# Layer 0 of a two-layer encoder: the Fourier input U taken in one folded pass at the end of the input projection

## The chip, the core and the metric

The kernel runs on one core of one Trainium2 chip. The metric is device time in microseconds (us) for one execution of the whole program; smaller is better. The program before takes 1407.87 us, the median of three runs (1405.26 to 1408.24).

## What is computed

Two layers (`DEPTH` 2) over 512 tokens of width 2048, in float32. Each layer makes shift, scale and gate from a condition vector `c`, normalises the tokens, projects them by `w_in`, mixes one half of the result with a Fourier transform and the other half with latent attention, and projects back by `w_out`:

```python
mod = c_act @ w_ada[l] + b_ada[l]
shift, scale, gate = jnp.split(mod, 3, axis=-1)
h = _layernorm(x) * (1.0 + scale[:, None, :]) + shift[:, None, :]
p = h @ w_in[l]
u_f, z_f, cq, ckv, k_r, z_a = jnp.split(p, split_pts, axis=-1)
y_f = _fourier_mix(u_f, w_fmix[l]) * jax.nn.silu(z_f)
...
y = jnp.concatenate([y_f, y_a], axis=-1) @ w_out[l]
x = _layernorm(DEEPNORM_ALPHA * x + gate[:, None, :] * y, ln_g[l], ln_b[l])
```

`_fourier_mix` takes the real part of a transform over the 512 tokens and the 128 channels of each of 8 groups, and then one 128 x 128 map per group. `w_in` has 3904 columns: 1024 of U (`u_f`), 1024 of ZF (`z_f`, the gate of the Fourier half), 512 of CQ, 320 of CKV with the rotary key, and 1024 of ZA (the gate of the attention half). The real part of a transform of real data is even, so tokens t and 512-t enter only by their sum and difference, and likewise channels c and 128-c. "Folded" means that sums and differences are formed first, which halves the products.

## The kernel before

**Products.** Every float32 product is made of three TensorE matmuls (`mm3`, lines 149 to 152): each operand is split into a rounded high part (`split`, line 146, a cast on ScalarE) and the rest (line 147, a subtraction on VectorE). A block of weights therefore costs a DMA, a ScalarE cast, a VectorE subtraction and matmuls. Blocks come through a `Stream` of units in program order, with two units converted and four loaded ahead (`st`), three raw buffers (`wrp`) and 35 buffers of 4 KB per partition (`bp`).

**Condition vectors.** `w_ada` (50 MB a layer) is not multiplied on TensorE. VectorE adds each row of a loaded tile, times one element of `c_act`, into an accumulator (`ada`, lines 244 and 246). The generator `background` holds this work in due order: shift and scale of layer 0 by blocks of 128 columns, layer 0's gate, then layer 1. `bg_step(n)` lets n pieces through, and the numbers ZP, ZL, AP and CP say how many per unit of weights in the steps of the projection, in the last step, in attention and in the output projection. The tiles are loaded into six buffers (`adp`); 160 pieces of 1024 columns have to be done by the end of layer 0.

**Input projection, layer 0.** The blocks of 128 input features are taken in five steps of 1, 2, 3, 4 and 6 (`SZ`), because a block's `h` needs its shift and scale. In each step all eight groups of columns (UA and UB, the two halves of U, then CQ, CKV, two of ZF, two of ZA) are multiplied by the step's blocks. UA stays in its four PSUM banks through all steps (`keep`); every other group is added to a sum in SBUF after each step (line 1120, VectorE). In the last step the order is UA, CQ, CKV, UB, ZF, ZA. U is folded over tokens after the projection (`folded`), and the transform (`fourier`, called through `pieces`) is dealt out between matmuls of the following groups, as are the latents (`latent_q`, `latent_kv`) and the rotary queries. The ZF gate is applied at once (`gate_f`).

**Input projection, layer 1.** All blocks are ready, and U is folded before the product: `fold_unit` forms sums and differences of weight columns (lines 397, 398) and a product for the token that has no partner (line 408), `u_pass` multiplies 16 blocks of sums and differences of tokens, `folded_constants` and `fourier_folded` make the transform, and `gates` applies ZF, which waited in DRAM (`szd`). Another group of matmuls runs between the pieces of the transform.

**Afterwards.** `project`, `scores`, `probs_T` and `weighted` are attention over 16 half heads; then the output projection in four groups of 512 columns (`residual`, line 1222, and `finish_rows`).

**Order.** A scheduler fixes each engine's instruction order, that of the DMA queues too, when the program is built; at run time every engine takes its instructions in that order and waits at each for what it needs.

## Time and profile before

| what | value |
|---|---|
| median of three runs | 1407.87 us (1405.26 to 1408.24) |
| the profiled execution: its time, its span | 1404.26 us, 1402.5 us |
| TensorE (PE) busy | 1344.3 us, 96% of the span |
| VectorE (DVE) busy | 1015.6 us, 72% |
| ScalarE (ACT) busy | 579.6 us, 41% |
| DMA | 253.24 MB, 181 GB/s over the span |
| step 4 of layer 0 begins on PE | at about 251 us |
| first maximum of layer 0's scores on DVE | at 436.95 us |

The profiled execution is 3.6 us below the median of the three runs. Busy time of an engine is the union of its instructions; durations of instructions overlap a little, so that the distance between two starts is less than a duration. Times in the trace count from the start of the span. The profile names a helper's line for each instruction, so that tiles and shapes tell which work it is: `acc<-ada` is the condition product, `b<-wr` a weight split, `b<-b,pm` with line 1120 a sum over steps.

### The profile page before, as it was taken

Reading aid. Unit: us, or ns where it says so; the run is one execution under the profiler, and the core shown is the slowest. Engines: PE = TensorE matmul, PEld = TensorE weight load, DVE = VectorE, ACT = ScalarE, POOL = GpSimd, SP = SyncE. Lnnn points to the kernel's source line nnn. Section 1 sums busy time; section 2 is a strip of 40 time slices with the busy share of each in tenths; the row PEclk is TensorE's granted clock in tenths of the full one; section 3 lists DMA queues with packets and bytes.
Section 4 is the critical chain, followed back from the end, with each engine's and each line's share of the span. In section 5 each row is a group of like instructions: output and inputs, shape, how many; then the busy total and the mean of one; then the engine's idle time right before and its main releaser. Section 6 shows DMA issues by size and latency. Waiting matters only on the chain. (4 is left out here: it accounts for less than half of the span.)

```text
span 1402.5 us, 18691 instructions
## 1 busy us (share of the span) xinstructions
PE 1344.3 (96%) x6949; PEld 1141.2 (81%) x6949; DVE 1015.6 (72%) x1670; ACT 579.6 (41%) x1052; POOL 55.5 (4%) x82
## 2 busy tenths in 40 slices
PE   4899999999999999999988999998999999999996
PEld 3688888787888888788877888887898888888885
DVE  7899999849978986658588748567655576642448
ACT  6722332224437776112167524323234677721210
POOL 1000000000000000000030001011000000000001
PEclk9999999999999999999998999999999999999998
DMA  9988898824764444968336435369444221263323
GB/s 288 299 293 300 271 349 286 306 76 122 211 206 140 157 128 161 317 199 283 105 145 203 161 96 166 105 205 367 152 119 121 74 67 54 80 236 105 91 60 120
DMA packets 134546, 253.24 MB, mean 181 GB/s; under 512 B 19308, under 2 KB 50168, under 8 KB 134456
## 3 DMA queue, kind: packets, MB, share of 16 engines
q1 hardware_dynamic: 127416, 228.73, 50.1%
q0 software_dynamic: 7040, 23.34, 4.9%
q8 instruction: 54, 0.88, 0.3%
q14 instruction: 36, 0.29, 0.1%
HBM read 237.32 MB, written 14.70 MB: 180 GB/s over the span
## 5 line engine op out<-in xcount | busy, mean ns | idle before, releaser
L150 PE MATMUL pa<-b,b 128*128 128x512 f32 (+4 forms) x1432 | 537.4, 377 | 11.6 <-ACT b L146 5.5
L151 PE MATMUL pa<-b,b 128*128 128x512 f32 (+4 forms) x1432 | 535.9, 375 | 4.3 <-DVE ln_v L187 4.3
L152 PE MATMUL pa<-b,b 128*128 128x512 f32 (+4 forms) x1432 | 534.5, 374 | 1.9 <-DVE b L147 1.9
L146 ACT CAST b<-wr 128x1024 fp32r<-128x1024 f32 (+3 forms) x184 | 180.0, 988 | 356.1 <-PE pa L152 181.1
L150 PEld LDWEIGHTS pa<-b,b 128*128 128x128 f32 x1432 | 271.2, 190 | 59.7 <-ACT b L146 9.2
L151 PEld LDWEIGHTS pa<-b,b 128*128 128x128 f32 x1432 | 272.1, 190 | 48.1 <-DVE ln_v L187 4.6
L152 PEld LDWEIGHTS pa<-b,b 128*128 128x128 f32 x1432 | 271.5, 190 | 48.2 <-DVE b L147 2.9
L147 DVE TENSOR_TENSOR b<-wr,b 128x1024 fp32r<-128x1024 f32 (+3 forms) x184 | 208.1, 1141 | 136.5 <-PE pa L151 84.7
L246 DVE SCALAR_TENSOR_TENSOR acc<-ada,cact,acc 128x1024 f32<-128x1024 f32 (+2 forms) x193 | 227.2, 1184 | 23.1 <-DMA ada<-in_w_ada_dram 21.2
L150 PE MATMUL pm<-b,b 128*128 128x512 f32 (+3 forms) x594 | 201.7, 341 | 1.2 <-ACT b L146 0.8
L151 PE MATMUL pm<-b,b 128*128 128x512 f32 (+3 forms) x594 | 197.2, 333 | 0.0
L152 PE MATMUL pm<-b,b 128*128 128x512 f32 (+3 forms) x594 | 197.0, 333 | 0.0
L150 PEld LDWEIGHTS pm<-b,b 128*128 128x128 f32 x594 | 111.7, 189 | 17.8 <-ACT b L146 2.7
L151 PEld LDWEIGHTS pm<-b,b 128*128 128x128 f32 x594 | 112.3, 189 | 10.5
L152 PEld LDWEIGHTS pm<-b,b 128*128 128x128 f32 x594 | 112.2, 189 | 10.4
L146 ACT CAST b<-pm 128x512 fp32r<-128x512 f32 (+4 forms) x110 | 54.9, 530 | 72.6 <-PE pm L800 17.8
L147 DVE TENSOR_TENSOR b<-pm,b 128x512 fp32r<-128x512 f32 (+4 forms) x110 | 64.1, 610 | 23.6 <-ACT b L146 23.0
L1120 DVE TENSOR_TENSOR b<-b,pm 128x512 f32<-128x512 f32 (+1 forms) x88 | 55.5, 656 | 4.5 <-PE pm L152 4.1
L146 ACT CAST b<-t 128x512 fp32r<-128x512 f32 (+1 forms) x73 | 35.9, 525 | 31.4 <-PE pm L151 9.5
L1039 DVE TENSOR_REDUCE mx<-pa 128x1 f32<-128x512 f32 x64 | 42.9, 684 | 5.3 <-PE pa L1037 4.7
L1044 ACT ACTIVATE t<-t,ssum 128x512 f32<-128x512 f32 x64 | 45.9, 735 | 1.2 <-DVE ssum L1043 1.2
L1042 ACT ACTIVATE t<-pa,mx 128x512 f32<-128x512 f32 x64 | 44.0, 693 | 4.6 <-DVE mx L1039 4.5
(186 smaller groups left out, 1120.7 us busy)
## 6 DMA issues: line engine op xcount, KB each, us to landing
wr<-in_w_in_dram SPq DMA_DIRECT2D x105, 512.0 KB, 4.6
ada<-in_w_ada_dram SPq DMA_DIRECT2D x96, 512.0 KB, 5.3
wr<-in_w_out_dram SPq DMA_DIRECT2D x64, 512.0 KB, 4.1
ada<-in_w_ada_dram SPq DMA_DIRECT2D x96, 256.0 KB, 4.9
ada<-in_w_ada_dram POOLq DMA_DIRECT2D x32, 512.0 KB, 5.4
b<-in_x_dram SPq DMA_DIRECT2D x16, 512.0 KB, 6.3
ada<-in_w_ada_dram SPq DMA_DIRECT2D x32, 192.0 KB, 5.3
wr<-in_w_q_b_dram SPq DMA_DIRECT2D x48, 128.0 KB, 3.0
```

Source lines behind the costliest of these rows:

```text
L146: A.copy(hi, src)
L147: V.tensor_tensor(lo, src, f(hi), op=ALU.subtract)
L150: PE.matmul(o, lh, rh, start=first, stop=False)
L151: PE.matmul(o, lh, rl, start=False, stop=False)
L152: PE.matmul(o, ll, rh, start=False, stop=last)
L246: V.scalar_tensor_tensor(out=a, in0=t[:, r - r0], scalar=cact[:, r:r + 1], in1=a, op0=ALU.mult, op1=ALU.add)
L1039: V.reduce_max(mx, ps, axis=AX.X, negate=True)
L1042: A.activation(e, ps, AF.Exp, bias=mx, accum_out=ssum)
L1044: A.activation(e, e, AF.Copy, scale=ssum)
L1120: V.tensor_tensor(s_[tb], s_[tb], banks[tb][:, :n], op=ALU.add)
```

## The change

In layer 0 U leaves the five steps. The steps multiply six groups; CQ instead of UA stays in banks until the last step (`FIRST`, `LAST`), from where ScalarE copies it out (`latent`). The tokens' transposed `xT` tiles are kept until the end. After the last step, 16 fold units follow; each one first makes its block of token sums and differences (`first_eo`, as the `act` of `fold_unit`), four units ahead (`UA0`). Then `u_pass` runs on all 16 blocks, and `fourier_folded` alternates with the rotary queries. Both gates go to DRAM and ZF comes back in `gates` during attention, where the splits of the Fourier result begin four rounds later (`YS`). The constants of the transform hold four of the six `adp` buffers in layer 0. The pace of the condition products is set anew: fewer in the projection, more in attention and in the output projection. The first residual waits for the gate vector by `gates_done`. `fourier_weights`, `fourier`, `folded`, `gate_f`, `silu` and `pieces` fall away. The diff, cut to its core:

```diff
-    ZP, ZL, AP, CP, G0, G1 = 0.5, 1.0, 1.0, 1.4, 0.8, 1.6
+    ZP, ZL, AP, CP, G0, G1 = 0.3, 0.5, 1.2, 2.3, 0.8, 1.6
...
-    FW, UAH = 2, 6
+    FW, UAH, UA0, YS = 2, 6, 4, 4
...
-    def fold_unit(src, k):
+    def fold_unit(src, k, act=None):
...
         def conv(t):
+            if act is not None:
+                h[k] = act(k)
...
-    FIRST = [UA, UB, CQ, CKV] + ZF + ZA
-    LAST = [UA, CQ, CKV, UB] + ZF + ZA
+    FIRST = [CQ, CKV] + ZF + ZA
+    LAST = [CQ, CKV] + ZA + ZF
...
+            for k in range(NK):
+                st.add(fold_unit(w_in[l], k, lambda k: first_eo(k)))
+            for k in range(2):
+                st.add(wq_unit(l, 4 * k, 4, 128, 64))
...
-            if n[0] <= 6:
+            if n[0] <= (6 if l else 4):
                 return adp.tile(shape, dt, tag="ada", name=nm("fc"))
...
+    def first_eo(k):
+
+        t, v = t2([P, S]), t2([P, S])
+        A.activation(t, xT[k // 2][:, k % 2], AF.Identity, scale=modT[0][:, 16 + k:17 + k], bias=modT[0][:, k:k + 1])
+        V.tensor_tensor(v[:, 0:256], t[:, 0:256], t[:, 256:512], op=ALU.add)
+        V.tensor_tensor(v[:, 256:512], t[:, 0:256], t[:, 256:512], op=ALU.subtract)
+        A.copy(orow[:, k:k + 1], v[:, 256:257])
+        hk = big([P, 2, S])
+        split(hk[:, 0], hk[:, 1], v)
+        return hk
...
-                pace = left[0] / (8.0 * len(pairs(k0, nk)) * LEADS[step])
+                pace = left[0] / (6.0 * len(pairs(k0, nk)) * LEADS[step])
...
-                fa = fourier(0, folded(k_group(UA, keep)))
-                pq = k_group(CQ, [pm() for _ in range(NT)])
...
+                lq = latent_q(k_group(CQ, keep))
                 next(lq)
...
+                lkv = latent_kv(k_group(CKV, pas(), runner(lq)))
                 next(lkv)
...
+                for i, (g, dst) in enumerate(zip(LAST[2:], (0, 1, 2, 3))):
+                    if i == 3:
+                        finish_late()
+                        st.ahead(4, UA0)
+                    zs = k_group(g, pas(), runner(lkv) if i == 0 else lambda: None)
+                    for j in range(4):
+                        A.activation(zs[j], zs[j], AF.Silu)
+                    spill(dst, zs)
+                drain(lkv)
+                cw, nq, dt = folded_constants(0)
+                u = u_pass()
+                st.ahead(4, 2)
+                fb, rq = fourier_folded(u), rotary_queries(1)
+                for i in range(8):
+                    next(fb, None)
+                    next(rq, None)
+                    next(fb, None)
                 drain(fb)
...
+                gt = gates()
...
-            if i < 4:
-                for k in range(2 * i, 2 * i + 2):
+            next(gt, None)
+            next(gt, None)
+            if YS <= i < YS + 4:
+                for k in range(2 * (i - YS), 2 * (i - YS) + 2):
...
-                if l == 1 and g == 0:
-                    drain(bg)
-                    finish_late()
+                if g == 0:
+                    while l not in gates_done:
+                        if stop[0]:
+                            finish_late()
+                        else:
+                            bg_step(1)
```

The diff does not tell where the scheduler puts this work. On DVE, at the end of layer 0's input projection, the order of before has the sums of the last group and then the rotary queries (`t` from `pm` with `cos_t`, `sin_t`):

```order
L1120 TENSOR_TENSOR b_627<-b_627,pa_3470 128x512
L1120 TENSOR_TENSOR b_627<-b_627,pa_3471 128x512
L975 TENSOR_TENSOR t_3613<-pm_3600,cos_t 128x4x32
L976 TENSOR_TENSOR t_3614<-pm_3600,sin_t 128x128
L978 TENSOR_TENSOR t_3613<-pm_3600,cos_t 128x4x32
```

In the change the fold units stand there, each with the split of its token sums (`b` from `t`), two folds of weights (`b` from `wr`), the product for the single token (`xacc`) and the split of the folded weights (`b` from `b`), here with a condition product (`acc` from `ada`):

```order
L148 TENSOR_TENSOR b_2892<-t_2887,b_2892 128x512
L401 TENSOR_TENSOR b_2895<-wr_2884 128x8x63
L402 TENSOR_TENSOR b_2895<-wr_2884 128x504
L412 SCALAR_TENSOR_TENSOR xacc_2610<-b_2895,orow,xacc_2610 128x520
L615 TENSOR_TENSOR t_3160<-t_3159 128x256
L247 SCALAR_TENSOR_TENSOR acc_1622<-ada_4077,cact,acc_1622 128x1024
L148 TENSOR_TENSOR b_2897<-b_2895,b_2896 128x1024
```

Four fold units stand ahead of the sums of the last ZF group, twelve behind them; among these twelve are five condition products.

On DVE behind the pass, the first pieces of the folded transform (`b` from `pm`, then `b` from `t` and `pm`) and the rotary queries alternate with condition products, of which 14 stand between the pass and the first maximum of the scores:

```order
L148 TENSOR_TENSOR b_3523<-pm_3535,b_3523 128x255
L925 TENSOR_TENSOR t_3512<-t_3512,t_3513 128x4x32
L247 SCALAR_TENSOR_TENSOR acc_4407<-ada_4660,cact,acc_4407 128x1024
L425 SCALAR_TENSOR_TENSOR t_3520<-t_3512,t_3520 128x4x64
L779 TENSOR_TENSOR b_3544<-t_3556,pm_3546 128x255
L780 TENSOR_TENSOR b_3544<-t_3556,pm_3546 128x255
L781 COPY b_3544<-t_3556 128x2
L247 SCALAR_TENSOR_TENSOR acc_4407<-ada_4726,cact,acc_4407 128x1024
```

In the order of before the transform's pieces stand earlier, between the weight splits of UB, ZF and CKV.

On DVE in the output projection of layer 0, in its second group, before has a weight split (`b` from `wr`) for every one or two condition products at most places:

```order
L246 SCALAR_TENSOR_TENSOR acc_5889<-ada_6264,cact,acc_5889 128x1024
L147 TENSOR_TENSOR b_5897<-wr_5830,b_5896 128x1024
L246 SCALAR_TENSOR_TENSOR acc_5889<-ada_6267,cact,acc_5889 128x1024
L147 TENSOR_TENSOR b_5930<-wr_5863,b_5929 128x1024
L147 TENSOR_TENSOR b_5980<-wr_5900,b_5979 128x1024
```

In the change three or four of them stand between two splits:

```order
L148 TENSOR_TENSOR b_5917<-wr_5834,b_5916 128x1024
L247 SCALAR_TENSOR_TENSOR acc_5771<-ada_5946,cact,acc_5771 128x1024
L247 SCALAR_TENSOR_TENSOR acc_5771<-ada_5949,cact,acc_5771 128x1024
L247 SCALAR_TENSOR_TENSOR acc_5771<-ada_5952,cact,acc_5771 128x1024
L247 SCALAR_TENSOR_TENSOR acc_5771<-ada_5985,cact,acc_5771 128x1024
L148 TENSOR_TENSOR b_5956<-wr_5870,b_5955 128x1024
```

Between the residuals of the first and of the third group stand 21 condition products before and 40 in the change.

## Rows read from the trace of the kernel before

**Rows 1.** The page, busy tenths in 40 equal slices of the span.

```profile
PE   4899999999999999999988999998999999999996
DVE  7899999849978986658588748567655576642448
```

**Rows 2.** Windows: stretch, its length, busy us by engine, granted clock, DMA share, GB/s.

```profile
core 0: us, PE busy (x) PEld busy (x) DVE busy (x) ACT busy (x) POOL busy (x), PEclk, DMA share, GB/s
60.00:250.00 190.00, 188.63 (x885) 158.81 (x884) 185.52 (x231) 52.68 (x66) 1.88 (x3) 1.00 0.90 303
250.00:437.00 187.00, 185.42 (x987) 156.47 (x986) 140.69 (x275) 76.53 (x154) 4.24 (x4) 1.00 0.54 172
437.00:545.00 108.00, 108.00 (x666) 95.11 (x665) 96.21 (x169) 84.92 (x177) 0.00 (x0) 1.00 0.44 139
590.00:635.00 45.00, 43.73 (x195) 35.99 (x196) 29.95 (x35) 7.61 (x8) 0.00 (x0) 1.00 0.67 230
635.00:680.00 45.00, 45.00 (x202) 37.27 (x200) 33.34 (x36) 8.58 (x9) 0.00 (x0) 1.00 0.65 229
```

**Rows 3.** DVE's groups by shape, 100 to 250 us: busy us, mean ns.

```profile
L246 DVE SCALAR_TENSOR_TENSOR acc<-ada,cact,acc 128x1024 f32<-128x1024 f32 x48 | 61.5, 1282 | 0.4
L1120 DVE TENSOR_TENSOR b<-b,pm 128x512 f32<-128x512 f32 x49 | 32.0, 683 | 1.3 <-PE pm L152 1.2
L147 DVE TENSOR_TENSOR b<-wr,b 128x1024 fp32r<-128x1024 f32 x22 | 26.8, 1222 | 0.2 <-PE pm L151 0.2
```

**Rows 4.** Timeline of PE, end of step 3: start us, duration us.

```profile
246.68 0.39 PE L150 MATMUL pm<-b,b 128*128 128x512 f32 x1
...
251.22 0.39 PE L152 MATMUL pm<-b,b 128*128 128x512 f32 x1
251.44 3.60 PE L518 MATMUL pm<-b,b 128*128 128x512 f32 x8
```

**Rows 5.** Timeline of DVE: products and sums at the end of step 3.

```profile
249.56 1.28 DVE L246 SCALAR_TENSOR_TENSOR acc<-ada,cact,acc 128x1024 f32<-128x1024 f32 x1
250.75 0.68 DVE L1120 TENSOR_TENSOR b<-b,pm 128x512 f32<-128x512 f32 x1
251.64 0.69 DVE L1120 TENSOR_TENSOR b<-b,pm 128x512 f32<-128x512 f32 x1 [0.21 <-PE pm L152]
```

**Rows 6.** Timeline of DVE: the first maximum of the scores.

```profile
436.95 0.69 DVE L1039 TENSOR_REDUCE mx<-pa 128x1 f32<-128x512 f32 x1 [0.54 <-PE pa L1037]
```

**Rows 7.** Timeline of PE in layer 1's folded pass, one block of 18 matmuls.

```profile
884.25 0.28 PE L150 MATMUL pa<-b,b 128*128 128x264 f32 x1
884.37 0.29 PE L151 MATMUL pa<-b,b 128*128 128x264 f32 x1
...
887.04 0.28 PE L150 MATMUL pa<-b,b 128*128 128x264 f32 x1
```

**Rows 8.** Timeline of DVE in layer 1's folded pass, one fold unit.

```profile
857.49 0.68 DVE L397 TENSOR_TENSOR b<-wr 128x504 f32<-128x504 f32 x1
858.08 0.68 DVE L398 TENSOR_TENSOR b<-wr 128x504 f32<-128x504 f32 x1
858.67 0.76 DVE L408 SCALAR_TENSOR_TENSOR xacc<-b,orow,xacc 128x520 f32<-128x520 f32 x1
859.95 1.23 DVE L147 TENSOR_TENSOR b<-b,b 128x1024 fp32r<-128x1024 f32 x1 [0.53 <-ACT b L146]
861.09 0.68 DVE L397 TENSOR_TENSOR b<-wr 128x504 f32<-128x504 f32 x1
```

**Rows 9.** DVE's groups by shape, 290 to 437 us.

```profile
L421 DVE SCALAR_TENSOR_TENSOR b<-wr,vecT,b 128x256 fp32r<-128x256 f32 x16 | 7.1, 482 | 0.0
L421 DVE SCALAR_TENSOR_TENSOR t<-t,t 128x256 fp32r<-128x256 f32 x8 | 3.4, 424 | 0.9 <-ACT t L420 0.5
L147 DVE TENSOR_TENSOR b<-pm,b 128x257 fp32r<-128x257 f32 x8 | 3.4, 422 | 5.3 <-ACT b L146 5.3
L729 DVE TENSOR_TENSOR b<-t,pm 128x255 f32<-128x255 f32 x8 | 3.3, 417 | 2.8 <-ACT t L728 2.8
L975 DVE TENSOR_TENSOR t<-pm,cos_t 128x128 f32<-128x128 f32 x8 | 2.3, 289 | 9.5 <-PE pm L152 9.5
```

**Rows 10.** Windows of 10 us in the output projection.

```profile
550.00:560.00 10.00, 10.00 (x50) 8.38 (x49) 5.93 (x9) 2.27 (x3) 0.00 (x0) 1.00 0.98 339
650.00:660.00 10.00, 10.00 (x46) 8.29 (x45) 9.86 (x9) 2.11 (x2) 0.00 (x0) 1.00 1.00 384
```

**Rows 11.** Windows of 5 us with PE partly idle.

```profile
55.00:60.00 5.00, 3.15 (x14) 2.26 (x14) 3.96 (x4) 5.00 (x9) 0.00 (x0) 1.00 0.83 265
740.00:745.00 5.00, 2.00 (x9) 2.00 (x10) 5.00 (x13) 0.36 (x1) 1.55 (x3) 0.50 1.00 359
```

More of the change, by code (lines that the diff above doesn't have):

```diff
@@ L229, in ada_tiles @@
         return t
-    late = []
+    late, gates_done = [], []
     def ada(l, pieces, cols, tiles=None):
@@ L452, in trunk_kernel @@
     ends = []
-    CQ, CKV, UA, UB = (CQ0, 512), (CKV0, 320), (U0, 512), (U0 + 512, 512)
+    CQ, CKV = (CQ0, 512), (CKV0, 320)
     ZF = [(Z0, 512), (Z0 + 512, 512)]
     ZA = [(ZA0, 512), (ZA0 + 512, 512)]
-    FIRST = [UA, UB, CQ, CKV] + ZF + ZA
-    LAST = [UA, CQ, CKV, UB] + ZF + ZA
+    FIRST = [CQ, CKV] + ZF + ZA
+    LAST = [CQ, CKV] + ZA + ZF
     def add_groups(src, groups):
@@ L467, in trunk_kernel @@
                 for g in FIRST if k0 + nk < NK else LAST:
-                    for i, (k, n) in enumerate(pairs(k0, nk)):
-                        if k0 + nk == NK and g == ZA[1] and i in (0, 4 // RN0):
-                            st.add(wq_unit(l, 4 * (i > 0), 4, 128, 64))
+                    for k, n in pairs(k0, nk):
                         st.add(dense(w_in[l], k * P, *g, n))
+            for k in range(NK):
+                st.add(fold_unit(w_in[l], k, lambda k: first_eo(k)))
+            for k in range(2):
+                st.add(wq_unit(l, 4 * k, 4, 128, 64))
         else:
@@ L507, in fm_half @@
                     first and i == 0, last and i == nr - 1)
-    def fourier_weights(l):
-        cw, dt = [[None, None], [None, None]], []
-        cc = big([P, 2, P], F32)
-        GP.dma_start(cc, chan.rearrange("a p c -> p a c"))
-        wf = big([P, G, P], F32)
-        SP.dma_start(wf, w_fmix[l].rearrange("g m d -> m g d"))
-        for hf in range(2):
-            for a in range(2):
-                ps = pm()
-                PE.matmul(ps, cc[:, a], wf[:, hf * 4:hf * 4 + 4].rearrange("p g d -> p (g d)"),
-                          start=True, stop=True)
-                t = big([P, 2, 512])
-                split(t[:, 0], t[:, 1], ps)
-                cw[a][hf] = t
-        for k in range(2):
-            t = big([P, 2, S])
-            for a in range(2):
-                GP.dma_start(t[:, a], dft[a, k * P:(k + 1) * P, :])
-            dt.append(t)
-        return cw, dt
     def folded_constants(l):
@@ L859, in drain @@
                 pass
-        def gate_f(zg, zs):
-            for j in range(4):
-                y = yf[zg * 2 + j // 2][:, j % 2]
-                V.tensor_tensor(y, y, zs[j], op=ALU.mult)
-        def silu(banks, dst=None):
-            zs = [t2([P, S]) if dst is None else dst[j] for j in range(4)]
-            for j in range(4):
-                A.activation(zs[j], banks[j], AF.Silu)
-            return zs
         def latent(src, n, nt):
-            if l == 0:
+            if l == 0 and nt == 320:
                 p = src
+            elif l == 0:
+                t = [big([P, 2, nt], F32) for _ in range(2)]
+                p = [t[tb // 2][:, tb % 2] for tb in range(NT)]
+                for tb in range(NT):
+                    A.copy(p[tb], src[tb])
             else:
@@ L1104, in k_group @@
                         left[0] -= p_
-                        bg_step(p_ if p_ > 0 else ZL if final else ZP)
+                        bg_step(p_ if p_ > 0 else 0 if g == LAST[-1] and final else ZL if final else ZP)
                         if g in ZF or g in ZA:
@@ L1110, in k_group @@
                         work()
-                    if g == UA:
+                    if g == CQ:
                         return banks
@@ L1126, in trunk_kernel @@
                     for i, g in enumerate(FIRST):
-                        k_group(g, keep if g == UA else [pm() for _ in range(NT)])
+                        k_group(g, keep if g == CQ else [pm() for _ in range(NT)])
                         if step == 0 and i == 3:
```

72 lines of the change are left out of this document (3 added, 69 removed).

## The prediction

> **What bounds the kernel now.** I read the page's slices first [rows 1]: PE is at nine tenths nearly everywhere, and in layer 0's input projection, slices 2 to 13, DVE is as full in most of the first seven. The windows make this sharp [rows 2]: from 60 to 250 us, steps 2 and 3 and what surrounds them, PE is busy 188.6 of 190 us and DVE 185.5, at full clock. So two engines bound this stretch, and a change must relieve both. From 250 to 437, the last step up to the first score, PE is still full and DVE has 46 us free; in attention, 437 to 545, PE alone is full. DVE's groups say what fills it [rows 3]: condition products of 1024 columns, sums over steps, and weight splits. Back to back they cost less than their durations: on the timeline a product lasts 1.28 us but the next starts 1.2 later, and a sum of 0.68 takes about 0.60 [rows 5]. On PE 21 matmuls of 512 columns start within 4.54 us, 0.227 us each [rows 4].
>
> **The change part by part.** All sums are made against the profiled execution, 1404.26 us; the median of three is 3.6 higher, so I add that at the end. About 2.8 us (0.2%) is what can be told from no change.
>
> *PE's work.* U costs 16 blocks x 24 matmuls x 0.227 = 87.2 us. The folded pass costs 16 blocks x 2.79 us, by layer 1's timeline [rows 7], = 44.6. Transform and constants come out even within a few us (23.6 before, about 22 by counting the new matmuls at the same prices). That makes 44 us less on PE: 10 blocks x 24 x 0.227 = 54.5 less before step 4, and about 10.5 more after it.
>
> *Term 1, up to step 4 at 252.3 us [rows 4, 5].* DVE can't give back 54.5, since it is full there [rows 2]. From it leave: the splits of ten blocks of U weights, 1.22 each [rows 3] less the overlap, 10 x 1.14 = 11.4; the sums of UB, which is gone, and of CQ, which stays in its banks, four each in three steps, 24 x 0.60 = 14.4; and condition products, 11 fewer by the order x 1.2 = 13.2. Together 39, and instruction by instruction 37.7. I take **-38**. At worst step 1, which is bound by ScalarE and loads, keeps its share, -30; at best ScalarE and DVE waits shrink with it, -43. xT's kept tiles cost one of six condition buffers' worth of room; with DMA at 0.90 of its share [rows 2] that belongs to the -30.
>
> *Term 2, from there to the first score maximum, 436.95 - 252.3 = 184.6 us before [rows 6].* Now: six groups of six blocks, each 12 x (5 x 0.227 + 0.14 for the short CKV), about 92, with transposes of latents 98. PE is the slower engine here. Then DVE, because its work comes in a chain: four fold units stand before the last sums, twelve behind. A layer-1 unit goes from start to start in 3.61 us, 0.53 of it a wait for ScalarE [rows 8]; here the split of the token sums, 0.60, is added: 4.2 us against PE's 2.79 per block. PE therefore waits about 1.4 us in each of twelve blocks, 17 us. Twelve units are 50.5, five condition products that fill their waits 5 x (1.2 - 0.53) = 3.4, last sums and constants 6.6; the halves of the token sums lie in ScalarE's waits. Weights of the rotary queries: 14 x 0.40, from 0.48 less the overlap [rows 9], = 5.6; copying out the pass about 17 instructions at 0.42 [rows 9], 7.1. From there to the first maximum DVE has 14 condition products (16.8), eight rounds of rotary queries at 1.55, one instruction of 0.42 and four of 0.29 (12.4), some 24 sums and splits of the transform (9.1) and 16 splits of the first heads' projection (6.4), at up to 0.42 apiece [rows 9], waits 3: 48. The sum is 98 + 60.5 + 12.7 + 48 = 219.2, or **+34.6**. If the twelve units run at PE's pace and the 19 condition products fall into gaps, it is about +18; if ScalarE, which now also forms tokens and rounds twice per unit, holds each unit by another 0.53, +41.
>
> The price of a unit rests on starts, not ends: each instruction of the unit but the last begins 0.09 us before the one ahead ends [rows 8]. The Trainium skill, "VectorE: DVE Perf Modes", section "The DRAIN you can't avoid", says that the next operation does not start until the pipe is empty, though it adds that one which is not held starts earlier. Read by its first half alone, twelve units of five instructions would take 60 x 0.09 = 5.4 us more, and the time would be some 1412; the trace bears out the second half.
>
> *Term 3, attention.* PE is full, 108 of 108, DVE at 96 [rows 2]. Eight gate products (8 x 0.6) come to DVE, five or six condition products go (-7). I set **0**; what hides it is DVE's 12 free us, and without that cover it would be at most 5.
>
> *Term 4, layer 0's output projection.* Between the residuals of the first and third group 40 condition products stand instead of 21. Their tiles of 0.524 MB, 21 MB, and 8.4 MB of `w_out` share SP's queue in about 87 us: 29.4 MB, 337 GB/s. Before, the two halves moved 230 GB/s at a share of 0.67 [rows 2]; single windows show 339 at 0.98 and 384 at 1.00 [rows 10]. So this is at the edge. DVE needs 19 x 1.2 = 23 us more, and has 45 - 30 and 45 - 33, 27 free. Neither is over its limit, both are near: **+2**, from 0 (hidden) to +10 (300 GB/s, as the front sustains).
>
> Removed instructions such as `fourier_weights`, and the spill of ZF, which goes through DRAM and comes back in attention at a DMA share of 0.44, I set at nothing.
>
> Sum: -38 + 34.6 + 0 + 2 = -1.4, that is 1402.9 for such an execution and **1406** by the median's scale. PE's 44 us come back as waits for DVE: 17 in the pass, some 27 in the tail up to the first maximum and in the front, where DVE gives up less than PE.
>
> **The rivals.**
> *A, DVE's chain is looser than its order.* The 19 condition products of term 2 are not needed until much later, and ScalarE's waits and the 46 free us of the last step [rows 2] may swallow them, as may an earlier start of units. For it: 12 waits of 0.53 and the spread of the order. Against it: a static order puts them between units. At the +18 end of term 2 the time is 1404.3 - 38 + 18 + 2 + 3.6 = 1390; cases in this direction spread from 1384 to 1400.
>
> *B, PE's whole saving shows*: 1408 - 44 = 1364. It needs DVE to keep up in the front, and [rows 2] speak against it.
>
> *C, slower: the output projection is bound by SP's queue.* The weights of the next group are queued behind condition tiles on SP, so PE waits for weights once 337 GB/s are more than the queue holds. The point from which it decides is the rate: at 303 [rows 2] 29.4 MB take 97 us, +10, and a first residual that waits for the gate adds a few; at 339 [rows 10] nothing. Against it: 384 was reached for 10 us. It gives 1406 + 8 to 12, about 1416.
>
> *D, slower: the clock falls in the pass.* PE is busy there 2.79 of 4.2 us, 3.3 of 5. The granted clock was 1.00 with 3.15 of 5 busy and 0.50, the 1.2 GHz level, with 2.00 of 5 [rows 11]; the pass lies at the upper one. At the lower level a block takes 5.6 instead of 4.2 us: 12 x 1.4 = 17 us, 1423. The Trainium skill, "TensorE: Matmul & The Clock Gate", section "A second HAM failure mode: psum-queue depth-cycling", reports a kernel in which short idle times between groups of matmuls made the clock swing between its levels. By that rule D would be the likely case; in the rows before, the clock is 1.00 at a like share, so I give it little.
>
> **How the numbers follow.** Forecast (1400 to 1412): 0.46, of it 0.14 faster, 0.20 the same, 0.12 slower. A 0.27 and B 0.03, faster. C 0.15, of it 0.02 the same. D 0.06 and 0.03 for mishaps unnamed, slower. Faster 0.44, same 0.22, slower 0.34. The range 1388 to 1421 leaves out B, the low end of A (0.06), the top of C and most of D: 0.18. The forecast's own range is 1400 to 1412.
>
> **What would show it.** Step 4 begins on PE near 214 us, with DVE full up to there (term 1); in the pass PE starts a block every 4.2 us or so, waiting for DVE's weight splits, at clock 1.00 (term 2); the first maximum of the scores stands near 434; PE stays full in attention; the output projection moves about 335 GB/s with short waits for weights. I am wrong if step 4 begins before 205 or after 222, if the pass runs at 2.8 to 3.2 us a block with the first maximum before 425 (A), if the output projection lengthens by 8 us or more (C), or if the clock in the pass is 0.50 (D).

## The result, and the profile after

The change takes 1414.13 us (median of 20 runs, 1408.34 to 1419.68) against 1405.68 for the kernel before (20 runs): a ratio of 1.0059, 95% interval 1.0046 to 1.0072. It is slower by 8 us, where 1406 and no change were forecast. The profiled execution of the change took 1409.84 us (span 1408.0), 5.6 more than that of before; the other 3 us of the medians are in no trace read here.

The time in us of the two profiled executions, cut at the forecast's own marks (the end of the last sum of step 3, the end of the pass on PE, the first score maximum, the first residual of the first and of the third output group, the end):

| stretch | before | after | difference | forecast |
|---|---|---|---|---|
| to the end of step 3 | 252.3 | 217.1 | -35.2 | -38 |
| to the first maximum | 184.6 | 224.8 | +40.1 | +34.6 |
| of it up to the pass's end | | 158.7 | | 158.5 |
| of it behind the pass | | 66.0 | | 60.7 |
| attention, to the first residual | 151.8 | 150.3 | -1.5 | 0 |
| first to third output group | 87.0 | 92.4 | +5.3 | +2 |
| rest | 726.7 | 723.5 | -3.2 | 0 |

The windows (columns as in [rows 2]; the first line is of before, the others of after) show the exchange. PE is no longer full in the front, where DVE nearly is; PE waits in the pass and behind it.

```profile
60.00:252.30 192.30, 190.93 (x893) 160.36 (x892) 187.61 (x234) 52.68 (x66) 2.95 (x5) 1.00 0.90 304
60.00:217.00 157.00, 146.43 (x667) 121.15 (x666) 148.87 (x186) 43.20 (x56) 1.92 (x2) 0.96 0.83 279
214.00:250.00 36.00, 35.69 (x189) 30.97 (x188) 16.92 (x49) 14.51 (x31) 2.12 (x2) 1.00 0.29 83
312.00:370.00 58.00, 49.51 (x274) 38.39 (x273) 55.09 (x88) 28.90 (x71) 2.99 (x5) 1.00 0.63 188
370.00:437.00 67.00, 53.12 (x338) 46.94 (x337) 58.43 (x143) 28.94 (x76) 0.00 (x0) 0.90 0.63 207
```

On DVE's timeline of after step 3 ends with the sum at 216.44 (before: [rows 5]); one weight split follows, and then DVE stands idle for 13 us. It waits for a cast on ScalarE, whose order has CQ's copies out of the banks ahead of it, and these wait 12.2 us for CQ's last matmul.

```profile
216.44 0.68 DVE L1063 TENSOR_TENSOR b<-b,pm 128x512 f32<-128x512 f32 x1
217.04 0.82 DVE L148 TENSOR_TENSOR b<-wr,b 128x640 fp32r<-128x640 f32 x1
231.31 0.83 DVE L148 TENSOR_TENSOR b<-wr,b 128x640 fp32r<-128x640 f32 x1 [13.46 <-ACT b L147]
```
```profile
227.35 0.59 ACT L820 COPY b<-pa 128x512 f32<-128x512 f32 x1 [12.19 <-PE pa L153]
```

The last sum of the last group on DVE's timeline, 94.7 us behind the end of step 3, waits for PE, the slower engine up to there:

```profile
311.86 0.69 DVE L1063 TENSOR_TENSOR b<-b,pa 128x512 f32<-128x512 f32 x1 [0.45 <-PE pa L153]
```

A unit of the pass on the same timeline, to be held against [rows 8]: from 324.38 to 329.50 it has a condition product, the second of its two token sums and the split of both, and DVE has no gap. It takes 5.1 us from start to start; other units with a product take 4.8, units without one 4.2 to 4.3.

```profile
324.38 0.68 DVE L401 TENSOR_TENSOR b<-wr 128x504 f32<-128x504 f32 x1
324.97 0.68 DVE L402 TENSOR_TENSOR b<-wr 128x504 f32<-128x504 f32 x1
325.56 0.75 DVE L412 SCALAR_TENSOR_TENSOR xacc<-b,orow,xacc 128x520 f32<-128x520 f32 x1
326.24 0.42 DVE L615 TENSOR_TENSOR t<-t 128x256 f32<-128x256 f32 x1
326.57 1.28 DVE L247 SCALAR_TENSOR_TENSOR acc<-ada,cact,acc 128x1024 f32<-128x1024 f32 x1
327.77 1.22 DVE L148 TENSOR_TENSOR b<-b,b 128x1024 fp32r<-128x1024 f32 x1
328.90 0.69 DVE L148 TENSOR_TENSOR b<-t,b 128x512 fp32r<-128x512 f32 x1
329.50 0.68 DVE L401 TENSOR_TENSOR b<-wr 128x504 f32<-128x504 f32 x1
```

Behind the pass (374.5 to 441.87 us) DVE's groups hold 16 condition products, and its waits there come to 9.6 us (waiter, whom for, total, times, longest); the first maximum is at 441.87 (before: [rows 6]).

```profile
L247 DVE SCALAR_TENSOR_TENSOR acc<-ada,cact,acc x15: 1262/1277/1282, 385.9 to 425.5; 128x1024 f32<-128x1024 f32 x15
L245 DVE TENSOR_SCALAR acc<-ada,cact x1: 753/753/753, 383.6 to 383.6; 128x1024 f32<-128x1024 f32 x1
```
```profile
DVE t L920 <- PE pm L153: 4.0, 6, 1.3
DVE b L148 <- ACT b L147: 3.0, 6, 0.9
DVE b L425 <- ACT b L424: 1.5, 2, 1.1
DVE t L425 <- ACT t L424: 1.1, 2, 0.5
```

The clock of after, in windows of 5 us: 1.00 all through the pass, where PE is busy some 3.5 of 5 us, and 0.50 behind it, after a stretch in which PE waits for the pass to be copied out. It falls in the front too, as it did not before, first at 90 us and again at 110 and at 165 us:

```profile
90.00:95.00 5.00, 1.75 (x4) 1.05 (x5) 4.96 (x7) 3.80 (x7) 0.00 (x0) 0.71 0.74 243
95.00:100.00 5.00, 5.00 (x15) 3.95 (x14) 5.00 (x6) 2.02 (x4) 0.00 (x0) 0.60 0.90 302
355.00:360.00 5.00, 3.58 (x21) 2.69 (x20) 5.00 (x8) 1.91 (x6) 0.00 (x0) 1.00 0.68 212
375.00:380.00 5.00, 0.83 (x6) 0.40 (x4) 4.59 (x11) 3.97 (x10) 0.00 (x0) 0.89 0.63 169
380.00:385.00 5.00, 3.87 (x17) 3.68 (x18) 4.32 (x15) 2.61 (x9) 0.00 (x0) 0.50 0.80 256
```

In the output projection the marks, which lie on DVE, say more than PE lost. Between the first residuals of groups 1 and 3 (before, then after) PE is idle 2.1 us before and 2.8 in the change, and in the change it has run 23 matmuls more by the records:

```profile
588.76:675.79 87.03, 84.90 (x377) 69.79 (x376) 60.35 (x66) 16.89 (x16) 0.00 (x0) 1.00 0.68 236
592.16:684.51 92.35, 89.56 (x400) 73.10 (x399) 84.32 (x88) 16.71 (x16) 0.00 (x0) 1.00 0.88 318
```

The third group's residual waited for PE before; in the change it stands, with no wait, behind a condition product (before, then after):

```profile
675.79 0.70 DVE L1222 TENSOR_TENSOR pa<-pa,t 128x512 f32<-128x512 f32 x1 [0.31 <-PE pa L152]
```
```profile
683.31 1.28 DVE L247 SCALAR_TENSOR_TENSOR acc<-ada,cact,acc 128x1024 f32<-128x1024 f32 x1
684.51 1.29 DVE L1159 TENSOR_TENSOR pa<-pa,t 128x512 f32<-128x512 f32 x2
```

So most of the +5.3 is a mark that comes late while PE works on, and the -3.2 of the rest takes part of it back.

### The profile page after: what moved, and what is told of

It is laid out like the page before. It is cut to its first block, busy times and chain, and to the rows that moved or that the text cites. A ratio compares the mean times of both kernels' runs of the same rounds, so it can differ in the third digit from the quotient of the medians.

```text
span 1408.0 us, 18682 instructions
## 1 busy us (share of the span) xinstructions
PE 1317.0 (94%) x6837; PEld 1114.3 (79%) x6837; DVE 1040.7 (74%) x1748; ACT 601.2 (43%) x1131; POOL 59.6 (4%) x87
## 5 line engine op out<-in xcount | busy, mean ns | idle before, releaser
L151 PE MATMUL pa<-b,b 128*128 128x512 f32 (+3 forms) x1472 | 549.4, 376 | 30.2 <-ACT b L147 16.3
L152 PE MATMUL pa<-b,b 128*128 128x512 f32 (+3 forms) x1472 | 549.3, 373 | 7.2 <-DVE ln_v L188 4.3
L153 PE MATMUL pa<-b,b 128*128 128x512 f32 (+3 forms) x1472 | 546.7, 372 | 0.5 <-DVE b L148 0.5
L151 PEld LDWEIGHTS pa<-b,b 128*128 128x128 f32 x1472 | 278.6, 191 | 83.5 <-ACT b L147 23.7
L152 PEld LDWEIGHTS pa<-b,b 128*128 128x128 f32 x1472 | 279.9, 190 | 54.1 <-DVE b L148 5.9
L153 PEld LDWEIGHTS pa<-b,b 128*128 128x128 f32 x1472 | 279.4, 190 | 47.6 <-DVE b L148 1.9
L147 ACT CAST b<-wr 128x1024 fp32r<-128x1024 f32 (+3 forms) x166 | 162.6, 991 | 325.8 <-PE pa L153 173.8
L148 DVE TENSOR_TENSOR b<-wr,b 128x1024 fp32r<-128x1024 f32 (+3 forms) x166 | 188.7, 1144 | 132.9 <-PE pa L152 68.6
L151 PE MATMUL pm<-b,b 128*128 128x256 f32 (+3 forms) x500 | 167.5, 335 | 7.2 <-DVE b L1063 5.7
L152 PE MATMUL pm<-b,b 128*128 128x256 f32 (+3 forms) x500 | 161.9, 324 | 0.0
L153 PE MATMUL pm<-b,b 128*128 128x256 f32 (+3 forms) x500 | 161.6, 323 | 0.0
L151 PEld LDWEIGHTS pm<-b,b 128*128 128x128 f32 x500 | 96.4, 193 | 19.5 <-issue 4.8
L153 PEld LDWEIGHTS pm<-b,b 128*128 128x128 f32 x500 | 96.4, 193 | 6.8
L152 PEld LDWEIGHTS pm<-b,b 128*128 128x128 f32 x500 | 96.5, 193 | 6.5
L148 DVE TENSOR_TENSOR b<-pm,b 128x512 fp32r<-128x512 f32 (+4 forms) x104 | 60.7, 606 | 22.7 <-ACT b L147 22.3
L147 ACT CAST b<-b 128x1024 fp32r<-128x1024 f32 (+1 forms) x48 | 43.2, 912 | 60.2 <-DVE b L402 50.0
L148 DVE TENSOR_TENSOR b<-b,b 128x1024 fp32r<-128x1024 f32 (+1 forms) x48 | 49.5, 1042 | 13.8 <-ACT b L147 13.8
L147 ACT CAST b<-t 128x512 fp32r<-128x512 f32 (+1 forms) x81 | 40.9, 531 | 26.3 <-DVE t L1021 13.7
L148 DVE TENSOR_TENSOR b<-t,b 128x512 fp32r<-128x512 f32 (+1 forms) x81 | 45.0, 576 | 8.2 <-ACT b L147 7.9
```

The costliest lines, as they stand in the source:

```text
L147: A.copy(hi, src)
L148: V.tensor_tensor(lo, src, f(hi), op=ALU.subtract)
L151: PE.matmul(o, lh, rh, start=first, stop=False)
L152: PE.matmul(o, lh, rl, start=False, stop=False)
L153: PE.matmul(o, ll, rh, start=False, stop=last)
```

## The experiments

Theory 1: behind step 3 VectorE's chain sets the end (units of the pass, then the tail from the pass's end to the first maximum), and the condition products that its order has there are paid in full. Rival 1: the tail is a chain of waits which the products only fill. Rival 2: the loss is the output projection's transfers. Rival 3: ScalarE or the loads set the units. In this section "first maximum" is that of layer 0's scores, "gaps" the two distances between the first residuals of output groups 1, 2 and 3, and "layer change" the way from the last row's residual of layer 0 to layer 1's first maximum. All marks come from DVE's timelines.

| run | first maximum | gaps | layer change | ratio to before (95%) |
|---|---|---|---|---|
| before | 436.95 | 43.7, 43.3 | 380.0 | |
| the change | 441.87 | 47.1, 45.2 | 378.1 | 1.0059 (1.0046 to 1.0072) |
| e1_hold | 430.15 | 42.6, 43.7 | 387.6 | 1.0007 (0.9995 to 1.0018) |
| e2_hold_zl2 | 446.35 | 45.3, 44.4 | 377.7 | 1.0006 (0.9993 to 1.0020) |
| e3_hold_zl3 | 454.05 | 44.0, 44.4 | 380.5 | 1.0045 (1.0029 to 1.0062) |
| e4_oldpace | 454.66 | 45.9, 42.6 | 398.2 | 1.0233 (1.0214 to 1.0253) |
| e5_eo12 | 429.60 | 42.6, 43.7 | 388.0 | 1.0014 (0.9998 to 1.0031) |
| e6_eo16 | 437.05 | 42.6, 43.7 | 391.4 | 1.0051 (1.0032 to 1.0069) |
| e7_eo12_ua6 | 434.28 | 42.5, 43.7 | 389.6 | 1.0057 (1.0037 to 1.0078) |
| e8_eo12_nohold | 447.22 | 46.6, 45.1 | 378.7 | 1.0077 (1.0048 to 1.0106) |
| e9_half | 426.25 | 42.6, 43.7 | 388.7 | 1.0007 (0.9989 to 1.0026) |
| e10_const | 435.29 | 42.6, 43.7 | 388.0 | 1.0042 (1.0024 to 1.0060) |
| e11_all | 423.29 | 44.2, 43.7 | 389.5 | 0.9958 (0.9944 to 0.9973) |
| e12_all_ua6 | 429.66 | 42.6, 43.7 | 388.4 | 1.0018 (1.0004 to 1.0031) |
| e13_poolq | 440.71 | 44.4, 43.1 | 379.2 | 1.0036 (1.0023 to 1.0050) |
| e14_all_zl1 | 428.62 | 45.3, 45.6 | 377.3 | 0.9865 (0.9842 to 0.9887) |
| e15_all_zl1_poolq | 423.88 | 45.7, 43.8 | 379.3 | 0.9941 (0.9925 to 0.9956) |
| e16_zl2_poolq | 448.90 | 45.6, 44.4 | 377.2 | 1.0105 (1.0087 to 1.0123) |
| e17_hold_zl1 | 430.59 | 45.3, 45.6 | 379.9 | 0.9933 (0.9915 to 0.9950) |
| e18_all_zl13 | 426.09 | 44.4, 46.1 | 380.7 | 0.9897 (0.9876 to 0.9919) |

The gaps and the end of attention have to be read with care, since a residual can stand on DVE behind condition products while PE works on. In e17_hold_zl1 the two gaps come to 90.9 us, 3.9 more than before, and PE is busy throughout:

```profile
578.51:669.45 90.94, 90.94 (x415) 75.54 (x414) 84.38 (x90) 17.06 (x17) 0.00 (x0) 1.00 0.89 335
```

**The products out of the tail.** The hold makes attention's condition products wait, on VectorE, for the last instruction of the first `project`:

```diff
+        if l == 0:
+            vh = [x for x in nc.cur_bb.bb.instructions if x.engine == V.engine][-1]
...
-                    bg_step(AP)
+                    with tc.issue_after(vh):
+                        bg_step(AP)
```

> The change with one edit: the condition products that attention lets through stand behind the last VectorE instruction of the first project. By the order, the products in the pass go from 5 to 0, those between the pass and the first maximum from 16 to 1, those from there to the first residual from 23 to 37. Theory 1 (VectorE's chain ends the pass and the tail behind it; in the trace of the change it waits only 11 of 67 us in the tail): 5 x 0.55 + 15 x 1.2 = 21 us of VectorE work leave the chain, some of it fills waits now; the first maximum comes at 422 to 430 instead of 441.9, and the time falls by 5 to 15 us, the rest is given back in attention, where VectorE then has 14 x 1.2 = 17 us more. Rival 1 (the tail is a chain of waits between TensorE, ScalarE and VectorE, which the products only fill): the first maximum moves by less than 4 us and the time by less than 3. Rival 2 (the loss is the output projection's condition tiles): the first maximum may move, but the groups of the output projection stay as far apart as in the change (47 and 45 us) and the time stays within 4 us of the change.

The first maximum came 11.7 us earlier, just past the late edge of the forecast (430), and the time fell by 8 us by the medians. Rival 1 allowed the first maximum less than 4 us and rival 2 the time 4 us, so both fall as they were stated. But theory 1 holds only in part: 20 products of 1.2 us, some 24 us of VectorE's time, left pass and tail, and half of that was gained. The pass ended 156.7 us behind step 3 instead of 158.7, and the tail took 55.7 us instead of 66.0. In the tail, now with one product, VectorE waits 15.1 us where it waited 9.6 with 16, so the products had filled some of the waits, as rival 1 says (columns as above):

```profile
DVE t L920 <- PE pm L153: 6.9, 6, 1.8
DVE b L148 <- ACT b L147: 3.1, 6, 1.6
DVE t L425 <- ACT t L424: 2.6, 5, 0.5
DVE b L779 <- ACT t L778: 1.5, 2, 1.1
DVE b L425 <- ACT b L424: 1.0, 1, 1.0
```

Part of what was won went elsewhere: the layer change took 9.5 us more (attention's 154.5 us instead of 150.3 ends at a residual that stands behind products, and says less). No theory had the cost at the layer change. Products that don't fit earlier are left over between the third output group and the end of layer 0 (11 in e1_hold from 671.6 us on, one in the change behind 685).

**Products in the last step.** ZL sets how many the last step lets through, CP how many the output projection does:

```diff
-    ZP, ZL, AP, CP, G0, G1 = 0.3, 0.5, 1.2, 2.3, 0.8, 1.6
+    ZP, ZL, AP, CP, G0, G1 = 0.3, 2.0, 1.2, 2.3, 0.8, 1.6
```

> As e1_hold, and ZL 2.0 instead of 0.5: by the order 22 condition products in the last step, where the change has none from 217 to 312 us and VectorE and DMA are partly free; 35 from the first maximum to the first residual, 18 and 9 in the first two gaps between residuals of the output projection instead of 19 and 21. Theory 1: first maximum as in e1_hold (422 to 430), the output projection 3 to 5 us shorter than the change's, time 1392 to 1402. Rival 1: first maximum at 438 to 446, time within 5 us of the change, less at most what the output projection gives. Rival 2: nearly all of a gain lies in the output projection, 5 us. A third way: the loads of the 22 tiles delay weights in the last step, whose end then moves by more than 5 us.

> As e2_hold_zl2 with ZL 3.0 and CP 1.4: by the order 37 condition products in the last step, 31 from the first maximum to the first residual, 16 and 0 in the gaps of the output projection. Theory 1: first maximum at 422 to 432, and the output projection as in the kernel before or shorter (gaps of 44 us): time 1388 to 1398. If VectorE or the loads fill up in the last step (37 x 1.2 = 44 us against some 40 free), the last step grows by 3 to 8 us and it is no better than e2_hold_zl2.

Theory 1's numbers failed in both, on the first maximum: it came 16 and 24 us later than in e1_hold. VectorE's free time in the last step did not take 22 or 37 products. In e2_hold_zl2 the first fold of weights starts at 305.1 instead of 287.9, and DVE waits there for the sums that its order has ahead (PE's last matmul of each):

```profile
296.32 0.69 DVE L1063 TENSOR_TENSOR b<-b,pa 128x512 f32<-128x512 f32 x1 [4.22 <-PE pa L153]
297.68 0.69 DVE L1063 TENSOR_TENSOR b<-b,pa 128x512 f32<-128x512 f32 x1 [0.67 <-PE pa L153]
```

**The pace of before.**

```diff
-    ZP, ZL, AP, CP, G0, G1 = 0.3, 0.5, 1.2, 2.3, 0.8, 1.6
+    ZP, ZL, AP, CP, G0, G1 = 0.5, 1.0, 1.0, 1.4, 0.8, 1.6
...
-                pace = left[0] / (6.0 * len(pairs(k0, nk)) * LEADS[step])
+                pace = left[0] / (8.0 * len(pairs(k0, nk)) * LEADS[step])
```

> The change with the pace of the condition products of the kernel before (0.5, 1.0, 1.0, 1.4 and 8.0), nothing held. By the order 8 products in the last step, 8 in the pass, 19 in the tail, 12 to the first residual, 15 and 8 in the gaps of the output projection, 9 in the third. Theory 1: pass and tail grow by 3 x 0.55 + 3 x 1.2 = 5 us, the output projection gives 4 to 5 back: within 3 us of the change. Rival 2 (the output projection's tiles are the loss): 5 to 6 us faster than the change.

Both were far off. It is 24 us slower than the change: 13 us are lost up to the first maximum and 20 at the layer change, and the stretches between give some back. At the layer change DVE has 16 products from 699 us on and PE is busy 5 of 20 us:

```profile
746.00:766.00 20.00, 5.23 (x23) 4.83 (x24) 15.56 (x32) 10.73 (x19) 9.09 (x11) 0.51 0.43 158
```

So the change's new pace is a needed part of it: with U's products gone from the front, what the front no longer covers must be done before layer 0 ends.

**Token sums ahead of the pass.** A generator step after each pair of blocks of the ZA and ZF groups:

```diff
+                            eo[len(seen)] = first_eo(len(seen))
...
-                st.add(fold_unit(w_in[l], k, lambda k: first_eo(k)))
+                st.add(fold_unit(w_in[l], k, lambda k: eo.pop(k) if k in eo else first_eo(k)))
```

> e1_hold, and the token sums and differences of the first 12 blocks, with their split, are made in the last step beside its matmuls, one after each pair of blocks of the ZA and ZF groups, and no longer in the fold units. Theory 1 (in the pass TensorE waits for VectorE's fold units): a unit loses a split of 0.60 and two sums of 0.34 that filled waits, so its period falls from 3.6 to 4.2 us to about 3.0 (0.59 + 0.59 + 0.69 + 1.15), near TensorE's 2.79; the last step has room on VectorE (some 45 us free between 217 and 312). The pass ends 8 to 12 us earlier, the first maximum at 418 to 423 instead of 430.2, the time is 1395 to 1400. Rival 3 (ScalarE's casts or the loads on SP's queue set the period of a unit): it stays at 3.5 or more, and the time within 3 us of e1_hold. Rival 4 (the six groups of the last step get longer by the work that moves in): the pass begins 5 us or more later and nothing is won.

> As e5_eo12 with all 16 blocks, two after each pair of blocks. Theory 1: as e5_eo12, 0 to 2 us better since no unit of the pass carries a split; if buffers run short (16 of 35 then hold token sums), weights come later and the last step grows by 3 us or more.

> As e5_eo12 with six instead of four units converted ahead at the end of the last step (UA0 6); by the order six fold units instead of four stand ahead of the last sums. Theory 1: two units of 3.0 us leave the pass, the first maximum 2 to 5 us earlier than in e5_eo12. If buffers run short, the groups of the last step wait for weights and it is no better.

> The change with the early token sums of e5_eo12 and without the hold; by the order 4 condition products in the pass and 16 in the tail. Theory 1: the pass as in e5_eo12 or 2 us longer, the tail as in the change (67 us from the pass's end to the first maximum): first maximum at 430 to 435, time 1403 to 1408. Rival 3: as the change, 1412 to 1416.

None paid, e8 included, whose first maximum came 12 us later than expected. In e5_eo12 the period of a unit fell to 3.6 us, not to 3.0: with the token sums gone, VectorE waits 0.5 us for ScalarE's cast instead (rival 3, in part). And the first unit behind the last group started 5 us later, at 325.9, because the constants waited for a buffer that a spill to DRAM held (below); with all 16 blocks the first fold came at 306.9 instead of 287.9.

```profile
317.68 0.30 DVE L535 COPY b<-b 128x64 f32<-128x64 f32 x2 [3.25 <-DMA szd<-b]
```

**The cast in two parts, and the constants earlier.** In layer 0's units:

```diff
-            split(hi, lo, w)
+            for hs in (slice(0, 520), slice(520, 1024)) if act is not None else (slice(0, 1024),):
+                split(hi[:, hs], lo[:, hs], w[:, hs])
```

and `cw, nq, dt = folded_constants(0)` moved ahead of the last ZF group.

> e1_hold with one edit: in layer 0's fold units the split of 1024 folded columns is made in two parts of 520 and 504, so that ScalarE can round the first part while VectorE still works on the single token's product. In the trace of e1_hold VectorE waits 0.50 us per unit for the cast of 1024 columns (period 4.2). Theory 1 (VectorE's chain of a unit sets the pass): the period falls by 0.3 to 0.5 us, one more instruction costs 0.1; over 12 units 3 to 5 us, first maximum at 425 to 428 instead of 430.2, time 2 to 5 us below e1_hold. Rival 4 (what sets the pass's end is the start of the chain, the constants, and loads): no change within 2 us.

> e1_hold with the constants of the transform formed ahead of the last ZF group instead of behind it. In the trace of e1_hold VectorE is taken by them and by waits for them from 314.9 to 321.6 us, while the pass waits for the fifth fold unit. Theory 5 (the place of the constants between last group and pass costs their 6 us): the fifth unit starts at 314 to 317 instead of 320.5, the first maximum comes 3 to 6 us earlier and so the time. If buffers run short the last group waits for weights instead, and nothing is won.

> e1_hold with the three edits together: 12 early token sums, two-part splits, constants ahead of the last group. Theories 1 and 5: units of 3.1 us from about 315, the pass bound by VectorE only a little (3.1 against 2.79), first maximum at 412 to 418, time 1388 to 1394. If one of them falls as in the runs alone, 1398 to 1404.

> As e11_all with six units ahead: by the order six fold units stand ahead of the last sums. If buffers allow it the pass starts with two more units ready, first maximum 2 to 5 us earlier than in e11_all; if not, the groups of the last step wait for buffers and it is later.

e9_half gave its 4 us by the profile, while its ratio can't be told from e1_hold's. e10_const lost: its first units came 20 us late. The three together gave what none gave alone. In e11_all a unit goes from start to start in 3.07 us with no wait, and PE is busy 10.0 of 10 us:

```profile
332.60 0.67 DVE L401 TENSOR_TENSOR b<-wr 128x504 f32<-128x504 f32 x1
333.19 0.67 DVE L402 TENSOR_TENSOR b<-wr 128x504 f32<-128x504 f32 x1
333.79 0.75 DVE L413 SCALAR_TENSOR_TENSOR xacc<-b,orow,xacc 128x520 f32<-128x520 f32 x1
334.46 1.28 DVE L148 TENSOR_TENSOR b<-b,b 128x520 fp32r<-128x520 f32 x2
335.66 0.67 DVE L401 TENSOR_TENSOR b<-wr 128x504 f32<-128x504 f32 x1
```
```profile
340.00:350.00 10.00, 10.00 (x65) 9.15 (x64) 10.00 (x17) 4.82 (x15) 0.00 (x0) 1.00 0.56 160
```

That shows directly that DVE's chain set the pass: with a shorter unit PE no longer waits. At 1397.8 us it still fell short of the 1388 to 1394 expected; the first maximum came 5 us late of the forecast, and the layer change kept its 10 us. Six units ahead cost again (e12_all_ua6: PE busy 6.45 of 10 us from 320).

**SP's queue.** The condition tiles of 1024 columns through POOL's queue:

```diff
-            (GP if l == 1 and c0 >= 32 * P else SP).dma_start(t[:, :, o:o + n],
+            (GP if l == 1 or c0 >= 32 * P else SP).dma_start(t[:, :, o:o + n],
```

> The change with one edit: the condition tiles of 1024 columns are loaded through POOL's queue, not SP's. If SP's queue (weights in order behind tiles that wait for a buffer) makes the output projection longer, its two gaps fall from 47.1 and 45.2 us to 43.6 to 44.5 and the time by 3 to 5 us; if the transfers themselves (317 GB/s there) or VectorE set it, the gaps stay within 1.5 us and the time within 3 us of the change. The first maximum stays within 3 us.

> e2_hold_zl2 with the tiles of 1024 columns through POOL's queue, 22 products in the last step as there. If SP's queue (weights behind condition tiles) made the fold units late in e2_hold_zl2: the first maximum falls from 446.4 to 430 to 436, and the time to 1398 to 1403. If the place of the products in VectorE's order made them late: first maximum at 443 to 449.

In e13_poolq the gaps fell by 4.9 us together, as expected if SP's queue sets them, and PE's idle time between these residuals fell from 2.8 to 0.2 us (columns as above):

```profile
591.09:678.56 87.47, 87.23 (x391) 71.73 (x391) 80.78 (x85) 17.94 (x17) 16.91 (x32) 1.00 0.92 338
```

But the gaps do not show that it is the queue. In the change SP waits 14.0 us, 16 times, for a free condition buffer in this stretch, with the weights of the next units queued behind. In e1_hold, whose tiles all stay on SP's queue, it waits 38.6 us, 30 times, and the gaps are 1.2 us shorter still, at 341 GB/s. The change, then e1_hold:

```profile
SPq L212 <- DVE acc L247: 14.0, 16, 1.9
```
```profile
SPq L212 <- DVE acc L247: 38.6, 30, 7.9
584.69:670.96 86.27, 84.25 (x375) 69.77 (x376) 78.46 (x82) 16.87 (x16) 0.00 (x0) 1.00 0.92 341
```

The medians of e13_poolq and of the change differ by 3.5 us, and their intervals overlap a little; what the queue costs by itself stays open. PE had 2.8 us of idle time to lose to it there. In the last step the queue is not what delays the units: e16_zl2_poolq was as late as e2_hold_zl2 (448.9). That leaves the other reading stated beforehand, the place of 22 products in VectorE's order.

**A few products in the 13 us gap.** ZL 1.0 puts 7 at the start of the last step, where DVE was idle, and takes as many from the end of layer 0.

> e11_all with ZL 1.0: by the order 7 condition products stand at the start of the last step, where VectorE waits 13 us (217 to 231) in the trace of the change, ahead of the token sums, and the rest is as in e11_all. If products are free in that gap: first maximum within 2 us of e11_all, 2 products fewer up to the first residual and 6 in the third gap gone, time 1395 to 1399. If their loads or their place delay the token sums and the units, as 22 products did, the first maximum is 3 to 6 us later.

> e14_all_zl1 with the tiles of 1024 columns through POOL's queue; by the order 42 products from the first maximum to the first residual instead of 35, 20 and 15 in the gaps. If SP's queue costs something in the last step or in the output projection: 2 to 5 us better than e14_all_zl1. If not, within 2 us, or worse by up to 4 where attention's VectorE work grows by 7 products.

> e1_hold with ZL 1.0: by the order 7 products in the gap at the start of the last step, 4 instead of 10 between the third residual group and the end of layer 0. In the traces so far the way from layer 0's last residual to layer 1's first maximum takes 388 to 390 us where 9 or 10 products stand in that third gap and 377 to 380 where 4 or fewer do. If those left-over products cost 10 us at the change of layers: 1393 to 1398, with the first maximum at 429 to 434 as in e1_hold. If the products in the last step delay the units: first maximum at 435 or later.

> e14_all_zl1 with ZL 1.3 and CP 2.0: by the order 12 products at the start of the last step, 18, 19 and 1 in the gaps of the output projection instead of 18, 20 and 4. If VectorE's gap there holds them (13 us for some 10): 1380 to 1385. If not, the token sums and units come later, as with 22 products: 1386 to 1394.

e17_hold_zl1, the change with nothing but the hold and ZL 1.0, takes 1395.4 us: its layer change is back at 379.9, its first maximum where e1_hold had it. With the three edits e14_all_zl1 takes 1384.06 us, ratio 0.9865 (0.9842 to 0.9887): faster than both kernels, and better than expected, since its layer change is 12.2 us shorter than that of e11_all. Three of its five executions lie near 1383.5 and two near 1390; the profiled one is of the two, with a front that is 7 us longer. From the end of step 3 to the first maximum it needs 204.3 us, against 213.7 in e17_hold_zl1 and 224.8 in the change. The seven products on DVE's timeline of e14_all_zl1, where the change waits:

```profile
224.98 6.56 DVE L247 SCALAR_TENSOR_TENSOR acc<-ada,cact,acc 128x1024 f32<-128x1024 f32 x5
231.69 0.75 DVE L245 TENSOR_SCALAR acc<-ada,cact 128x1024 f32<-128x1024 f32 x1 [0.15 <-DMA ada<-in_w_ada_dram]
233.00 1.28 DVE L247 SCALAR_TENSOR_TENSOR acc<-ada,cact,acc 128x1024 f32<-128x1024 f32 x1 [0.55 <-DMA ada<-in_w_ada_dram]
239.06 0.82 DVE L148 TENSOR_TENSOR b<-wr,b 128x640 fp32r<-128x640 f32 x1 [4.78 <-ACT b L147]
```

Twelve products there (e18_all_zl13) gain nothing more. POOL's queue costs 13 us here (e15_all_zl1_poolq). With it 42 instead of 35 products stand between the first maximum and the first residual, and so it is in e16_zl2_poolq against e2_hold_zl2. The residual comes late, and PE waits for the bank that it frees, 8.8 us in e16_zl2_poolq and 9.2 in e15_all_zl1_poolq:

```profile
PE pa L151 <- DVE b L1178: 9.2, 1, 9.2
```

In e14_all_zl1 and e2_hold_zl2 PE has no such wait there. No run has the queue without the other order.

## Why the prediction was wrong

- **The front: right in kind, 2.8 us too hopeful (term 1).** DVE limits it. From 60 us to the end of step 3 DVE's busy time fell by 38.7 us, about the 38 of the forecast, but its idle time grew from 4.7 to 8.1 us; the first 60 us are alike, and the time fell by 35.2. The -38 took such waits as unchanged. PE's clock, at 1.00 before, is 0.96 over this stretch.
- **The pass: right, and partly by luck.** Its end was forecast 158.5 us behind step 3 and came 158.7 behind, with units of 4.2 to 5.1 us that DVE fills; e11_all shows that it is DVE. But PE was done with the six groups after some 95 us instead of 98, and the chain behind took some 64 instead of 60.5.
- **The step that failed: the tail of term 2.** "Waits 3" was put for the way from the pass to the first maximum; measured are 9.6 us of DVE waits, 16 products instead of the 14 that were read from the order, and 66.0 us instead of 60.7. The pieces of the transform and the queries were summed up as one queue of work, but DVE waits for PE or ScalarE after many of them. e1_hold shows the size: with one product left the tail takes 55.7 us, 15.1 of them waits, where the same sum with one product gives 45.1. The products were priced at their full time and cost little more than half of it, which hid half of this error.
- **Term 4, +2 forecast, +5.3 by its marks.** PE's own idle time between them grew by 0.7 us only; the rest is DVE's residual standing behind products. So "neither is over its limit, both are near" was about right, and rival C's price of 8 to 12 us too high. Whether its mechanism, weights behind condition tiles on SP's queue, makes up the little there is, is not shown.
- The forecast's sum missed by 6.9 us: terms 1, 2 and 4 were too hopeful by 2.8, 5.5 and 3.3 us by the marks; attention (-1.5) and the rest (-3.2) took some back. The profiles differ by 5.6 us where -1.4 was forecast.
- **Rival A was half right.** The 20 products were indeed not needed where they stood, and about half of their time lay in waits, as it said. The other half was paid: without them the first maximum comes 11.7 us earlier. It took an edit, because run time does not change the order.
- **Rival B fell**: PE was busy 27.3 us less (1344.3 before, 1317.0 after) and the span is 5.5 us longer, so what PE saved came back as waits. **Rival D fell in its place**: in the pass, PE busy 3.5 of 5 us, the clock stayed at 1.00. What the Trainium skill, "TensorE: Matmul & The Clock Gate", section "A second HAM failure mode: psum-queue depth-cycling", reports of short idle times did not come about there. The clock fell elsewhere: behind the pass to 0.50, the 1.2 GHz level, after a stretch with 0.83 of 5 us busy, and in the front, after one with 1.75 of 5. What this adds to the tail and to the front was not tried.
- That an instruction starts only when the one ahead has ended, the reading that term 2 set aside, is not borne out here either: in e11_all each instruction of a unit again starts some 0.08 us before the one ahead ends.

Open stays what makes left-over products cost 10 us at the layer change. The count and the time go together in all runs (377 to 381 us with 4 or fewer by the traces, 388 to 398 with 11 or more), and e17_hold_zl1 differs from e1_hold by ZL alone. Over 40 us from shortly before the last group's first residual DVE is busy 38.4 us in e1_hold (692 to 732) and 32.1 in e17_hold_zl1 (688 to 728), so the left-over products may be paid in full there; which instruction is late was not tried by itself.

## What to carry to other kernels

Work that nothing waits for still costs time where a static order puts it between the instructions of a chain: here 20 products of 1.2 us made the chain 11.7 us longer, half of their time, and the other half filled waits. Read where it stands, not only whether the engine has room. A chain of short pieces over three engines is longer than the sum of one engine's pieces; its waits have to be summed too. Moving it pays in the amounts that a gap really has: here 7 instructions into 13 us of idle time, no cost, 22 into the same stretch, 16 us lost. And of three edits (an input made early, a cast in two parts, constants made early) one gave 4 us alone, one nothing and one lost 5; together they gave 7. A mark on one engine can come late while another works on, so check it against the idle time of the engine that bounds the kernel.

## What the runs showed of the hardware

A cast of 1024 columns on ScalarE held VectorE 0.5 us in each unit (e5_eo12, units of 3.6 us); cast in two parts of 520 and 504 columns, the wait is gone and a unit takes 3.07 us (e11_all). The same stretch of the output projection moved 318 GB/s in the change and 338 with the tiles on a second queue (e13_poolq), but 341 with all of them on the one queue (e1_hold), so no run shows that a second queue raises the rate. In the change's pass the granted clock was 1.00 from 340 to 365 us, where PE was busy some 3.5 of every 5 us, with idle pieces of 0.65 to 0.85 us.
